# Rotary embedding on one core: two stores move from ScalarE's DMA ring to SyncE's

## The chip, the core and the metric

The kernel runs on one NeuronCore of a Trainium2 chip. The metric is the device time of one execution in microseconds, as a median over runs. A profile of one execution gives the span on the core, which is shorter than the device time by what lies around it.

The engines that matter here are ScalarE (ACT in the profile), VectorE (DVE) and SyncE (SP). SyncE does no arithmetic; it issues DMAs. ScalarE and SyncE each have a DMA ring of their own: q10 is ScalarE's, q1 is SyncE's. Both rings are served by the same 16 DMA engines.

## What is computed

```python
def reference(x, cos, sin, num_heads):      # x: 16 x 512 x 1024 f32, 16 heads
    x = x.reshape(batch, seq, num_heads, head_dim)          # head_dim 64
    x1, x2 = x[..., :half_dim], x[..., half_dim:]           # half_dim 32
    cos = cos[None, :, None, :]                             # 512 x 32
    sin = sin[None, :, None, :]
    rotated = np.concatenate([x1 * cos - x2 * sin,
                              x1 * sin + x2 * cos], axis=-1)
    return rotated.astype(np.float32)
```

The input has 33.55 MB and the output as much. The two tables are 64 KB each.

## The kernel before

The 16 batches are cut into 8 slabs of 4.19 MB. A slab lies in the on-chip memory as 128 partitions of 8192 f32 values (32 KB a partition). The tile `room` has 6 such slots, and slab s uses slot s modulo 6, so slabs 6 and 7 reuse the slots of slabs 0 and 1.

**Loads.** The dictionary `loads` lists six DMAs: loads 0, 1, 6 and 7 bring one slab each, loads 2 and 4 bring two (2 and 3, 4 and 5). A one-slab DMA moves 32 KB rows and a two-slab DMA 64 KB rows. All are issued by SyncE (line 71). Loads 0, 1, 2 and 4 are issued at the start. Load 6 may only be issued when store 0 has landed, because it overwrites slab 0's slot; load 7 likewise after store 1.

**Stores.** The dictionary `stores` lists seven: stores 0, 1, 2, 3, 6 and 7 of one slab and store 4 of two (4 and 5). All are issued by ScalarE (line 174), each after the last copy back of its slabs. In the source, the loads that the store makes room for follow right behind it in the same loop body.

**Tables.** The cosine and sine tables come in through ScalarE's ring (line 87), are spread over the partitions by eight small matmuls (line 128), and end as bf16 tables `tab` (line 133).

**Compute.** A pass is a slab, or half a slab for slabs 0, 6 and 7. In each pass ScalarE casts the slab in place from f32 to bf16 (line 144), VectorE makes two products with the tables (line 165) and their sum (line 168), and ScalarE copies the sum back to f32 into the slot (line 170). The cast of the next pass stands in the source ahead of the copy back of the present one, so the cast of a slab can hold up the copy back, and so the store, of the slab before it.

**Order.** The program that results keeps one instruction stream for each engine. Each stream is in a fixed order, though not always in the source's: in the trace ScalarE casts slab 1 before it copies slab 0 back, and it issues store 2 behind the cast of slab 4. An instruction that waits holds up all that stands behind it on its engine. DMAs of one ring are worked off in the order in which they were issued.

Of the kernel before, what the change touches and what calls it, by code (L numbers as in the profile page):

```python
# [2 lines left out]

# [4 lines left out]


@with_exitstack  # L10
def kernel(
    ctx: ExitStack,
    tc: tile.TileContext,
    x: bass.AP,
    cos: bass.AP,
    sin: bass.AP,
    num_heads: int,
    out: bass.AP,
):
    nc = tc.nc  # L20
    P = nc.NUM_PARTITIONS

    batch, seq, dim = x.shape
    nh = num_heads
    hd = dim // nh
    half = hd // 2
    bf16 = mybir.dt.bfloat16
    f32 = mybir.dt.float32

    nb = 2  # L30
    slots = 6
    nslabs = batch // nb
    G = 2
    rpp = nb * seq // P
    W = rpp * dim
    SP = seq // rpp
    TW = rpp * half

    out_flat = out.rearrange("b s h d -> b s (h d)")

    singles = ctx.enter_context(tc.tile_pool(name="singles", bufs=1))
    psum = ctx.enter_context(tc.tile_pool(
        name="psum", bufs=1, space=bass.MemoryType.PSUM))


    def dram(t, s, k):
        return bass.AP(tensor=t.tensor,
                       offset=t.offset + s // G * (G * nb * seq * dim) + s % G * W,
                       ap=[[G * W, P], [1, k * W]])


    def view(t, offset, *dims):
        return dataclasses.replace(t, offset=t.offset + offset,
                                   ap=[t.ap[0], *[list(d) for d in dims]])


    room = singles.tile([P, slots * W], f32, tag="room")
    halves = room.bitcast(bf16)


    def slab(s, k):
        return view(room, s % slots * W, (1, k * W))


    loads = {0: 1, 1: 1, 2: 2, 4: 2, 6: 1, 7: 1}
    stores = {0: 1, 1: 1, 2: 1, 3: 1, 4: 2, 6: 1, 7: 1}


    def load(s):
        k = loads[s]  # L70
        nc.sync.dma_start(out=slab(s, k), in_=dram(x, s, k))  # L71

    TR = 32
    TQ = seq // TR // rpp
    TC = seq * half // TR
    raw = singles.tile([P, TC], f32, tag="raw")
    nc.vector.memset(raw, 0.0)  # L79


    def load_tables(queue):
        for i, src in enumerate((cos, sin)):
            to = dataclasses.replace(
                raw, offset=raw.offset + i * raw.ap[0][0],
                ap=[[P // TR * raw.ap[0][0], TR], [1, TC]])
            queue.dma_start(out=to, in_=bass.AP(
                tensor=src.tensor, offset=src.offset, ap=[[TC, TR], [1, TC]]))


    load(0)
    load_tables(nc.scalar)
    for s in loads:
        if 0 < s < slots:
            load(s)

    GP = SP // G
    GT = G // TQ  # L100
    pick = singles.tile([P, 3 * GT * P], bf16, tag="pick")
    nc.gpsimd.memset(pick, 0.0)  # L102


    def selection(g, h):
        return pick[:, (g * GT + h // TQ) * P:(g * GT + h // TQ + 1) * P]


    for g in range(3):
        for h in range(0, G, TQ):  # L110
            part = view(selection(g, h), 0, (GP, P // GP), (1, GP))
            nc.gpsimd.affine_select(  # L112
                out=part, in_=part, compare_op=mybir.AluOpType.not_equal,
                fill=-1.0 if g == 2 else 1.0,
                base=-(1 if g else 0) - h // TQ * (P // TR),
                pattern=[[0, P // GP], [-(G // TQ) * (P // TR), GP]],
                channel_multiplier=1)

    raw_b = singles.tile([P, TC], bf16, tag="raw_b")
    nc.gpsimd.tensor_copy(out=raw_b, in_=raw)  # L120

    tab = {}


    def table(h):
        acc = psum.tile([P, 2 * rpp * hd], f32, tag=f"acc{h}")
        for g, at in ((0, 0), (0, half), (2, rpp * hd), (1, rpp * hd + half)):
            nc.tensor.matmul(  # L128
                view(acc, at, (hd, rpp), (1, half)), selection(g, h),
                view(raw_b, h % TQ * TW, (half, rpp), (1, half)),  # L130
                start=True, stop=True)
        tab[h] = singles.tile([P, 2 * rpp * hd], bf16, tag=f"tab{h}", name="tab")
        nc.vector.tensor_copy(out=tab[h], in_=acc)  # L133

    def span(u):
        s, r, n = u
        at, m = s % slots * W + r * dim, n * dim
        return (m, view(room, at, (1, m)), view(halves, 2 * at, (1, m)),
                view(halves, 2 * at + m, (1, m)))


    def cast(u):
        m, full, low, high = span(u)
        nc.scalar.copy(out=low, in_=full)  # L144

    passes = []
    for s in range(nslabs):  # L150
        n = rpp if 1 <= s < nslabs - 2 else rpp // 2
        passes += [(s, r, n) for r in range(0, rpp, n)]


    cast(passes[0])
    for i, u in enumerate(passes):
        s, r, n = u
        if s < G and r == 0:
            table(s)
        if i + 1 < len(passes):  # L160
            cast(passes[i + 1])
        m, full, low, high = span(u)
        turned = view(low, half, (hd, n * nh), (-half, 2), (1, half))
        for out_, in_, a in ((high, turned, rpp * hd), (low, low, 0)):
            nc.vector.tensor_mul(  # L165
                out=out_, in0=in_,
                in1=view(tab[s % G], a + r * hd, (hd, n), (0, nh), (1, hd)))
        nc.vector.tensor_add(out=high, in0=low, in1=high)  # L168

        nc.scalar.copy(out=full, in_=high)  # L170
        if r + n == rpp:
            for t, k in stores.items():
                if t + k - 1 == s:
                    nc.scalar.dma_start(out=dram(out_flat, t, k), in_=slab(t, k))  # L174
                    for v in range(t + slots, t + k + slots):
                        if v in loads:
                            load(v)


# [1 line left out]
_INS = ['x', 'cos', 'sin', 'num_heads']  # L181
_OUTS = [((16, 512, 16, 64), 'float32')]

_NUMBERS = {'num_heads': 16}


# [26 lines left out]
```

## Time and profile before

| what | value |
|---|---|
| median of 3 runs | 162.29 us (162.16 to 162.79) |
| the profiled execution, device time | 162.28 us |
| its span | 160.5 us |
| ScalarE cast f32 to bf16, whole slab (L144) | 7.02 us |
| ScalarE copy back, whole slab (L170) | 7.01 us |
| ScalarE, half a slab, either | 3.60 us |
| VectorE, the two products and the sum of a slab (L165, L168) | 8.88 and 4.43 us |
| loads issued by SyncE | 0.74, 1.16, 1.64, 2.10 (loads 0, 1, 2, 4), 70.21 (6), 90.72 (7) |
| loads, us from issue to landing | 12.6, 21.7, 43.3, 71.7, 23.7, 23.0 |
| stores issued by ScalarE | 36.93, 58.88, 73.86, 87.77 (0 to 3), 115.17 (4), 129.35 (6), 143.52 (7) |
| stores, us from issue to landing | 33.2, 31.8, 35.0, 33.2, 25.1, 20.6, 16.1 |

Times of issue are microseconds from the span's start. A DMA's landing is its issue plus the time to landing; a DMA that stands in a ring behind others counts that queueing as part of it. In the profile's lines an item such as "ACT room L144 <- DMA room<-in_x_dram: 20.9, 4, 9.4" means that line 144 on ScalarE waited for the load of x, 20.9 us in total, 4 times, 9.4 us at most. The row "DMA" of the page gives the busy share of the 16 DMA engines in 40 equal slices of the span, in tenths.

### The profile page before, as it was taken

What the parts mean: (1) busy time and instruction counts of PE and PEld (TensorE: products, weight loads), DVE (VectorE), ACT (ScalarE), POOL (GpSimd) and SP (SyncE); (2) the same over time, 40 slices, a digit from 0 to 9 for tenths busy, and PEclk for the clock granted to TensorE, in tenths of its full rate; (3) what the DMA queues carried; (4) which work ended last, traced back from release to release, by engine and by line L of the source; (5) the groups of instructions that cost most, each with busy time, mean ns of one, the idle gap of its engine ahead of it and who ended that gap; (6) DMA issues with size and microseconds to landing.
All of it is one profiled execution on the core that took longest, in us unless ns stands there. A gap on an engine that the chain in (4) does not pass through costs nothing.

```text
span 160.5 us, 162 instructions
## 1 busy us (share of the span) xinstructions
PE 1.9 (1%) x8; PEld 1.1 (1%) x8; DVE 109.9 (68%) x36; ACT 113.3 (71%) x23; POOL 2.1 (1%) x9
## 2 busy tenths in 40 slices
PE   0004000000000000000000000000000000000000
PEld 0002000000000000000000000000000000000000
DVE  1002999999900999899789989999649999800000
ACT  3006939991089999997999999929999999170000
POOL 3001000000000000000000000000000000000000
DMA  7999999969599999999999999999996996999994
GB/s 261 408 408 392 523 392 523 506 278 523 245 408 392 555 490 392 392 392 392 465 441 400 433 474 400 433 474 400 408 604 294 523 490 294 400 474 433 392 474 180
DMA packets 1968, 67.24 MB, mean 419 GB/s; under 512 B 240, under 2 KB 240, under 8 KB 304
## 3 DMA queue, kind: packets, MB, share of 16 engines
q1 hardware_dynamic: 864, 33.55, 49.4%
q10 hardware_dynamic: 1104, 33.69, 48.6%
HBM read 33.69 MB, written 33.55 MB: 419 GB/s over the span
## 4 chain that ended last, share of the span: by engine, by line
ACT 36%; DMA 27%; DVE 13%; issue 12%; another core or an unknown queue 1%; SPq 0%; ACTq 0%
DMA room<-in_x_dram 27%; ACT room L170 22%; ACT room L144 14%; DVE room L165 8%; DVE room L168 4%; SPq L71 0%; ACTq L174 0%; ACTq L170 0%
## 5 line engine op out<-in xcount | busy, mean ns | idle before, releaser
L165 DVE TENSOR_TENSOR room<-room,tab 128x4096 bf16<-128x4096 bf16 (+1 forms) x22 | 71.6, 3259 | 15.0 <-ACT room L144 14.6
L144 ACT CAST room<-room 128x4096 bf16<-128x4096 f32 (+1 forms) x11 | 56.6, 5153 | 20.9 <-DMA room<-in_x_dram 20.9
L170 ACT CAST room<-room 128x4096 f32<-128x4096 bf16 (+1 forms) x11 | 56.6, 5154 | 6.6 <-DVE room L168 6.6
L168 DVE TENSOR_TENSOR room<-room 128x4096 bf16<-128x4096 bf16 (+1 forms) x11 | 35.9, 3261 | 0.3
L133 DVE CAST tab<-acc 128x1024 bf16<-128x1024 f32 x2 | 2.4, 1219 | 13.6 <-PE acc L128 13.6
L144 ACT ACT_TABLE_LOAD x1 | 1.3, 1283 | 2.7 <-issue 2.7
L128 PE MATMUL acc<-raw_b,pick 128*128 128x256 bf16 x8 | 1.9, 415 | 13.9 <-POOL raw_b L120 13.9
L128 PEld LDWEIGHTS <-pick 128*128 128x128 bf16 x8 | 1.1, 140 | 14.2 <-issue 12.2
L79 DVE MEMSET raw<- 128x512 f32 x1 | 0.5, 485 | 0.9 <-PEq L194 0.9
L112 POOL TENSOR_SCALAR_AFFINE_SELECT pick<-pick 128x128 bf16<-128x128 bf16 x3 | 0.8, 309 | 0.1
L120 POOL CAST raw_b<-raw 128x512 bf16<-128x512 f32 x1 | 0.6, 610 | 11.2 <-DMA raw<-in_sin_dram 11.2
L102 POOL MEMSET pick<- 128x384 bf16 x1 | 0.4, 418 | 0.3 <-POOLq L194 0.3
L194 POOL MEMSET const-float32-0.0<- 128x1 f32 x1 | 0.1, 98 | 0.2 <-issue 0.2
L194 POOL MEMSET const-bfloat16-1.0<- 128x1 bf16 x1 | 0.1, 101 | 0.0
L194 POOL MEMSET const-uint8-127<- 128x1 uint8 x1 | 0.1, 101 | 0.0
L194 POOL MEMSET const-float32-1.0<- 128x1 f32 x1 | 0.1, 98 | 0.0
## 6 DMA issues: line engine op xcount, KB each, us to landing
out_dram<-room ACTq DMA_DIRECT2D x6, 4096.0 KB, 32.5
room<-in_x_dram SPq DMA_DIRECT2D x4, 4096.0 KB, 22.3
raw<-in_cos_dram ACTq DMA_DIRECT2D x1, 64.0 KB, 7.9
raw<-in_sin_dram ACTq DMA_DIRECT2D x1, 64.0 KB, 11.1
room<-in_x_dram SPq DMA_DIRECT2D x2, 57.5
out_dram<-room ACTq DMA_DIRECT2D x1, 25.1
```

Of the source, the lines that this page charges most:

```text
L79: nc.vector.memset(raw, 0.0)
L102: nc.gpsimd.memset(pick, 0.0)
L112: nc.gpsimd.affine_select(out=part, in_=part, compare_op=mybir.AluOpType.not_equal, fill=-1.0 if g == 2 else 1.0, base=-(1 if g else 0) - ...
L120: nc.gpsimd.tensor_copy(out=raw_b, in_=raw)
L128: nc.tensor.matmul(view(acc, at, (hd, rpp), (1, half)), selection(g, h), view(raw_b, h % TQ * TW, (half, rpp), (1, half)), start=True, sto ...
L133: nc.vector.tensor_copy(out=tab[h], in_=acc)
L144: nc.scalar.copy(out=low, in_=full)
L165: nc.vector.tensor_mul(out=out_, in0=in_, in1=view(tab[s % G], a + r * hd, (hd, n), (0, nh), (1, hd)))
L168: nc.vector.tensor_add(out=high, in0=low, in1=high)
L170: nc.scalar.copy(out=full, in_=high)
L194: nc = _bacc.Bacc("TRN2", target_bir_lowering=False, num_devices=1)
```

## The change

Stores 0 and 1 are issued by SyncE in place of ScalarE, so that they enter SyncE's ring behind loads 0, 1, 2 and 4. The other five stores remain with ScalarE. Loads 6 and 7 still follow in SyncE's ring, each still waiting until the store of its slot has landed.

```diff
@@ -171,7 +171,8 @@
         if r + n == rpp:
             for t, k in stores.items():
                 if t + k - 1 == s:
-                    nc.scalar.dma_start(out=dram(out_flat, t, k), in_=slab(t, k))
+                    queue = nc.sync if t < 2 else nc.scalar
+                    queue.dma_start(out=dram(out_flat, t, k), in_=slab(t, k))
                     for v in range(t + slots, t + k + slots):
                         if v in loads:
                             load(v)
```

No instruction is added or removed, and the bytes moved are the same.

## The prediction

> **What bounds the kernel now.** I read the page's rows over time first, then the DMA queues in windows, the timeline around the last slabs, the waits and the DMA issues.
>
> ```profile
> span 160.5 us, 162 instructions
> PE 1.9 (1%) x8; PEld 1.1 (1%) x8; DVE 109.9 (68%) x36; ACT 113.3 (71%) x23; POOL 2.1 (1%) x9
> ...
> DMA  7999999969599999999999999999996996999994
> ...
> HBM read 33.69 MB, written 33.55 MB: 419 GB/s over the span
> ```
>
> No engine is busy for more than 71% of the span, but the DMA row stands at 9 nearly throughout. A slab is 4.19 MB. Store 6 was issued at 129.35 and landed 20.6 us later, at 149.95; store 7 at 143.52 and 16.1 us, so 159.62. So a slab takes 9.67 us when nothing is beside it (434 GB/s). From load 0's landing (0.74 + 12.6 = 13.3) the remaining 62.9 MB at 434 GB/s end at 158.4, and the last store landed at 159.6: the DMA lost 1.2 us in all, and the digit 5 (slice 40.1 to 44.1 us, just after the first store's issue at 36.9) says where. The kernel is bound by bytes; what can change the time is whether the DMA engines run dry.
>
> How the two rings share, by the DMA view in two windows (queue, packets, MB, share): 46 to 68 us, then 76 to 92 us. q1 is SyncE's ring, q10 ScalarE's.
>
> ```profile
> q1 hardware_dynamic: 96, 6.29, 65.9%
> q10 hardware_dynamic: 96, 3.15, 33.1%
> ```
> ```profile
> q1 hardware_dynamic: 112, 3.67, 53.1%
> q10 hardware_dynamic: 112, 3.15, 45.5%
> ```
>
> Packets alternate one for one: 96 to 96 while loads 2 and 4 (two slabs, 64 KB rows) meet one-slab stores (32 KB rows), so the load takes two thirds; 112 to 112 where both have 32 KB rows, about half each. With both rings at work a slab needs 2 x 9.67 = 19.3 us.
>
> The timeline where slabs 4 to 6 pass (start, us, line):
>
> ```profile
> 94.57 7.01 ACT L170 CAST room<-room 128x8192 f32<-128x8192 bf16 x1
> 94.69 8.88 DVE L165 TENSOR_TENSOR room<-room,tab 128x8192 bf16<-128x8192 bf16 x2 [0.49 <-ACT room L144]
> 101.49 3.60 ACT L144 CAST room<-room 128x4096 bf16<-128x4096 f32 x1
> 103.61 4.43 DVE L168 TENSOR_TENSOR room<-room 128x8192 bf16<-128x8192 bf16 x1
> 107.95 4.61 DVE L165 TENSOR_TENSOR room<-room,tab 128x4096 bf16<-128x4096 bf16 x2
> 108.12 7.02 ACT L170 CAST room<-room 128x8192 f32<-128x8192 bf16 x1 [3.04 <-DVE room L168]
> ...
> 115.17 0.34 ACTq L174 DMA_DIRECT2D out_dram<-room  x1
> ```
>
> ScalarE's order here is: copy back slab 4 (L170), cast the first half of slab 6 (L144), copy back slab 5, issue store 4 (slabs 4 and 5). The cast of slab 6 needs load 6 and stands in front of store 4. It waits for nothing now: load 6 was issued at 70.21 and landed 23.7 us later, at 93.9. Store 4 reaches its ring at 115.17, and store 3 ahead of it lands at 87.77 + 33.2 = 121.0: 5.8 us in hand.
>
> What waits, engines first, then SyncE:
>
> ```profile
> ACT room L144 <- DMA room<-in_x_dram: 20.9, 4, 9.4
> ```
> ```profile
> SPq L71 <- DMA out_dram<-room: 87.4, 2, 67.3
> ```
>
> SyncE issues four loads by 2.8 us and then sits: load 6 waits for store 0 (landed 36.93 + 33.2 = 70.1), load 7 for store 1 (58.88 + 31.8 = 90.7).
>
> **The change, part by part.**
>
> Two issues leave ScalarE and go to SyncE. Each took 0.34 us of ScalarE's sequencer at 36.93 and 58.88; after the first ScalarE waits for load 2 until 44.91 anyway, the second runs under a cast. Removing them is worth 0, and SyncE has idle time for two issues of 0.33 to 0.7 us. On SyncE the wait for slab 0's copy back now stands before store 1, load 6 and load 7, which all need it or come later.
>
> Loads 2 and 4 lose their competitor. Load 1 landed at 22.86; two slabs more give load 2 at 42.2 (before 44.9) and load 4 at 61.5 (before 73.8). ScalarE follows: cast of slab 2 at 42.2, copy back of slab 1 until 56.1 (store 1 can be issued 2.8 us earlier), cast of slab 3 until 63.1, copy back of slab 2 until 70.0, store 2 issued at 70.0 (before 73.86). The compute gains about 3.9 us here, which nothing at the end needs.
>
> Store 0 starts behind load 4 and has the engines alone: it lands at 61.5 + 9.7 = 71.2 (before 70.1). Load 6 is issued then, 1.1 us later than before. That is not its price: store 1 has been in SyncE's ring since 56.1 and stands ahead of it, while store 2, then store 3 (issued by 84), fill ScalarE's ring. From 71.2 each ring moves two slabs at 19.3 us: SyncE's store 1 and load 6, ScalarE's stores 2 and 3. All end at about 71.2 + 38.7 = 109.9. **Load 6 lands at 109.9 instead of 93.9.** This is the step that costs.
>
> ScalarE would come to the cast of slab 6 at about 98 (101.5 less the gain) and waits 12 us for load 6. Behind it on ScalarE stand the copy back of slab 5, whose data VectorE has by 105, and store 4; VectorE waits too. Cast 109.9 to 113.4, copy back to 120.4, store 4 issued at 120.4 (before 115.2), its first packets some 1.2 us later: 121.6. (No packet moved in the first microsecond, 6 did from 1.0 to 1.9 and 9 more to 2.4, after load 0's issue at 0.74.) Meanwhile the only work left is load 7: after load 6 it needs 9.7 us, so its data end at 118.9 (landing 119.6; I estimate 0.7 us from data to landing, as the 434 GB/s run into 159.6 leaves it). **The DMA runs dry from 118.9 to 121.6, 2.7 us.** Bounds: 0, if SyncE's ring gets some 7% more than half so that load 6 is early and store 3 is left over for the gap; 3.3, if first packets come 1.6 us after the issue (upper end of load 0's row) and the landing costs 0.2 more. I take 2.7, since both windows above show equal packets.
>
> After the gap stores 4, 6 and 7 run back to back: store 6 would be issued near 134.5 and store 7 near 148.6, before their predecessors end (141 and 150.6). Nothing makes up for the gap.
>
> The 1.2 us of loss at 40 to 44 is uncertain. Either it belongs to the first store of all (it then stays, near 61) or to a store ring starting against a load in flight (it then vanishes, as store 0 now follows loads in their own ring, unless store 2's start costs the same). Bounds 0 and -1.2; no row tells them apart, so I take -0.6.
>
> Sum: 160.5 + 2.7 - 0.6 = 162.6 us of span. The profiled execution took 162.28, 1.8 around its span, and the median is 162.29: **164.4 us**. Own range 163.2 to 165.5.
>
> **The rivals.**
>
> *The ring does not matter.* Total bytes and rate are fixed, and 429 and 426 GB/s moved in windows whether two-slab loads or stores were the partner. If load 6 lands by 107 (its cast then frees store 4 for 118.9), the engines never run dry: 162.3. For it: 5.8 us were in hand. Against it: load 6 has 16 us of extra queueing. The Trainium skill, "DMA: Bandwidth & Descriptors", section "Issuing engines are not separate DMA queues", speaks for this rival: DMAs of all issuing engines run on the same 16 engines and interleave, and choosing another issuer only saves sequencer time. By it the sum would be 162.3. The trace agrees on the rate; the order within a ring is what the rule says nothing of.
>
> *Faster.* The 1.2 us vanish and load 6 lands by 107: 162.3 - 1.2 = 161.1. It decides at the same point, 2.7 us less for load 6, and needs the loss to belong to two rings meeting.
>
> *Another order of instructions.* ScalarE's order in the trace is not the source's (the cast of slab 1 starts at 22.86, before the copies of slab 0 at 29.79), so the new program's order is a guess. If SyncE gets store 0, load 6, store 1, load 7, as the source's loop reads, store 1 is issued only after store 0 landed, lands near 110, and load 7 follows only then, beside store 4 with its 64 KB rows: 8 rounds of 3.63 us (1.21 + 2.42) put load 7 at some 141. From the cast of slab 7 (122.06) to store 7 (143.52) it is 21.5 us, then about 12 for a lone store as for load 0: 174.5, time 177. If instead ScalarE copies slab 5 back before it casts slab 6, store 4 meets load 7 in the same way, and the end is near 172.5, time 175. Against the first: the change as described puts both stores behind four loads and loads 6 and 7 after them. Against the second: it needs ScalarE's order to change, though only SyncE's instructions move.
>
> **How the numbers follow.** Forecast 0.70 (164.4); the ring does not matter 0.11 (162.3); faster 0.08 (161.1); another order 0.11 (175 to 177). The range goes down to include the neutral case, and up beyond the forecast's own; it leaves out the other orders and most of the faster case: 161.8 to 166.5. About 0.5% (0.8 us) is what a measurement of this kernel can tell from no change. Faster: 0.08 and a little of the neutral case, 0.09. Same: 0.10 of the neutral case and 0.04 of the forecast's low end, 0.14. Slower: the rest, 0.77.
>
> **What would show it.** Load 2 landing near 42, load 4 near 61.5, store 0 near 71. SyncE issuing store 1 at 56 and load 6 at 71. Load 6 landing near 110, and the cast of slab 6 (L144) idle for about 12 us before it, released by the load. Store 4 issued near 120.4, and the DMA row with a lower digit in the slice at 118 to 122. Wrong is the prediction if load 6 lands before 107, if SyncE's order differs, or if store 4 is issued before that cast.

## The result and the profile after

| kernel | median of the runs | ratio to before, 95% interval | span of the profiled execution |
|---|---|---|---|
| before | 162.29 us (162.13 to 162.79, 7 runs) | | 160.5 us |
| changed | 162.88 us (162.77 to 163.06, 7 runs) | 1.0036 [1.0026, 1.0045] | 161.2 us |

The change costs 0.6 us, which the interval sets clearly apart from nothing, though it is under the 0.5% that was named as the least this kernel's measurement can tell. The forecast was 164.4.

The page of the changed kernel, with the lines that answer to those of before: the DMA row, the bytes, then the two waits.

```profile
span 161.2 us, 165 instructions
...
DMA  7999999969969996999999999999989969999996
...
HBM read 33.69 MB, written 33.55 MB: 417 GB/s over the span
```
```profile
ACT room L144 <- DMA room<-in_x_dram: 12.0, 2, 9.6
```
```profile
SPq L71 <- DMA out_dram<-room: 30.6, 2, 21.0
```

The bytes are the same. The page counts 165 instructions instead of 162: the three more are waits for semaphores, one on SyncE and two on ScalarE, and the arithmetic and the DMAs are unchanged. The 5 that stood at 40 to 44 us has gone; a 6 stands at 44 to 48 us and another at 60 to 64 us, and an 8 at 117 to 121 us. A single low digit says little while 64 KB packets are counted by their start; the windows below decide. ScalarE waits less for loads (12.0 instead of 20.9 us in total). There is no 12 us wait in front of the cast of slab 6. The timelines of ScalarE say why. Before, from the cast of slab 2 to the copy back of slab 2:

```profile
44.91 7.02 ACT L144 CAST room<-room 128x8192 bf16<-128x8192 f32 x1 [8.02 <-DMA room<-in_x_dram]
51.84 7.01 ACT L170 CAST room<-room 128x8192 f32<-128x8192 bf16 x1
...
58.76 7.01 ACT L144 CAST room<-room 128x8192 bf16<-128x8192 f32 x1
...
65.68 7.01 ACT L170 CAST room<-room 128x8192 f32<-128x8192 bf16 x1
```

The changed kernel, from the copy back of slab 1 to the issue of store 4, with three rows of VectorE that the copies back of slabs 2 and 3 wait for:

```profile
44.30 7.02 ACT L170 CAST room<-room 128x8192 f32<-128x8192 bf16 x1 [7.25 <-DVE room L168]
51.22 20.85 ACT L144 CAST room<-room 128x8192 bf16<-128x8192 f32 x3
58.27 13.22 DVE L165 TENSOR_TENSOR room<-room,tab 128x8192 bf16<-128x8192 bf16 x3 [14.06 <-ACT room L144]
71.41 4.42 DVE L168 TENSOR_TENSOR room<-room 128x8192 bf16<-128x8192 bf16 x1
...
75.91 7.02 ACT L170 CAST room<-room 128x8192 f32<-128x8192 bf16 x1 [3.84 <-DVE room L168]
80.19 4.42 DVE L168 TENSOR_TENSOR room<-room 128x8192 bf16<-128x8192 bf16 x1
...
84.70 7.02 ACT L170 CAST room<-room 128x8192 f32<-128x8192 bf16 x1 [1.77 <-DVE room L168]
84.73 7.36 ACTq L175 DMA_DIRECT2D out_dram<-room  x2
92.14 7.02 ACT L144 CAST room<-room 128x8192 bf16<-128x8192 f32 x1 [0.41 <-ACT room L170]
...
105.98 7.11 ACT L144 CAST room<-room 128x4096 bf16<-128x4096 f32 x2
...
112.99 7.01 ACT L170 CAST room<-room 128x8192 f32<-128x8192 bf16 x1
...
120.04 0.34 ACTq L175 DMA_DIRECT2D out_dram<-room  x1
```

Before, ScalarE alternated: cast slab 2, copy slab 1 back, cast 3, copy 2 back, cast 4 and store 2, and so on. Now it copies slab 1 back first, at 44.30, then casts slabs 2, 3 and 4 in one go (51.22 to 72.07), and only then copies slabs 2 and 3 back. VectorE gets slab 2 later for it and begins at 58.27 (before at 51.96); it makes the two products of slab 2 and one of slab 3 before the sum of slab 2 (71.41), where before that sum followed its own products. So the copy back of slab 2 starts at 75.91, when the sum is done, 3.84 us after the last of the three casts. Store 2 stands behind the copy back of slab 3 as well and is issued at 84.73, just after the sum of slab 3 is done (80.19 + 4.42 = 84.61). Stores 2 and 3 are issued at 84.73 and 91.75 instead of 73.86 and 87.77. Moving two DMAs to another engine has thus changed the order of two engines whose arithmetic the diff does not touch; why the new order came out so is not shown. SyncE's order is the forecast's: loads 0, 1, 2, 4, stores 0 and 1, loads 6 and 7.

Four answers of the DMA view, each of a window around one issue, in the changed kernel: load 6 (issued at 72.70), load 7 (82.78), store 2 (84.73) and store 4 (120.04). The last number is the time to landing.

```profile
room<-in_x_dram SPq DMA_DIRECT2D x1, 4096.0 KB, 23.1
...
room<-in_x_dram SPq DMA_DIRECT2D x1, 4096.0 KB, 32.4
...
out_dram<-room ACTq DMA_DIRECT2D x1, 4096.0 KB, 23.2
...
out_dram<-room ACTq DMA_DIRECT2D x1, 20.8
```

With store 2 at 84.73, store 1 had the engines to itself and landed at 51.34 + 31.4 = 82.7. Load 6 followed at once and landed at 95.8, not at 109.9 as forecast. Store 4 needed 20.8 us to land: two slabs alone take 2 x 9.67 = 19.3, so next to nothing was ahead of it. Before it needed 25.1 us, because store 3 was still under way. This is a sign that the DMA engines may have run dry; the windows show it.

Where the time went is seen in the DMA columns of the windows (last two numbers: busy share, GB/s). They count a packet in the window in which it starts: GB/s times the window's length gives the bytes started, and share times length the time that those packets took on each of 16 engines. Before, then the changed kernel:

```profile
36.00:38.00 2.00, 0.00 (x0) 0.00 (x0) 2.00 (x1) 0.90 (x1) 0.00 (x0) 1.00 1.21 524
...
39.00:42.00 3.00, 0.00 (x0) 0.00 (x0) 2.97 (x2) 0.00 (x0) 0.00 (x0) 1.00 1.20 350
```
```profile
58.00:59.00 1.00, 0.00 (x0) 0.00 (x0) 0.73 (x1) 1.00 (x2) 0.00 (x0) 1.00 3.72 1049
...
120.00:120.85 0.85, 0.00 (x0) 0.00 (x0) 0.85 (x1) 0.85 (x2) 0.00 (x0) 1.00 0.01 0
120.85:122.00 1.15, 0.00 (x0) 0.00 (x0) 1.15 (x2) 1.15 (x1) 0.00 (x0) 1.00 2.14 912
```

Each of the first three windows holds 1.05 MB, 16 packets of 64 KB, one for each engine. In the first they took 1.21 x 2 = 2.42 us, in the second 1.20 x 3 = 3.60, in the third 3.72. So the last load packets ahead of the first store are stretched by 1.2 us before and 1.3 us after: the stretch has moved with the first store, from 39 to 58 us, and has not vanished. In the window from 120.00 to 120.85 of the changed kernel next to no packet starts. Packets of store 3 that started earlier still run in it; behind them the engines wait for store 4's first packets, 0.31 us on the mean.

From the packets' records I add up, for the kernels of this table, how much longer than usual the packets took (usual is 1.21 us for 32 KB and 2.42 for 64 KB) and how long engines had no packet, as a mean over 16 engines. The first microseconds and the last are left out. The labels e1 to e10 are the experiments of the next section.

| kernel | stretched, us | no packet, us | both, less before | span, less before |
|---|---|---|---|---|
| before | 1.20 | 0 | 0 | 0 |
| changed | 1.39 + 0.26 (near 87) | 0.31 (near 121) | +0.8 | +0.6 |
| e1, rings new, order old | 1.17 | 1.52 (near 121) | +1.5 | +1.3 |
| e2, rings old, order new | 1.16 | 3.55 (near 122) | +3.5 | +3.5 |
| e4, store 4 sooner | 1.5 | 2.45 (near 151) | +2.7 | +2.6 |
| e8, store 0 alone, order old | 1.25 | 0 | 0 | -0.1 |
| e9, as e1, store 2 later | 1.16 | 0 | 0 | -0.2 |
| e10, as e1, store 4 first | 1.6 | 5.82 (near 140 and 153) | +6.2 | +6.0 |

The two sums give each span to about 0.2 us. For the changed kernel they are 0.31 us without a packet and 0.45 us of longer packets, against 0.6 us of span. So the question for each kernel is where the DMA engines run dry, and where packets are stretched.

### The profile page after: what moved, and what is told of

Read it like the earlier page. It is cut to its first block, busy times and chain, and to the rows that moved or that the text cites. A ratio compares the mean times of both kernels' runs of the same rounds, so it can differ in the third digit from the quotient of the medians.

```text
span 161.2 us, 165 instructions
## 1 busy us (share of the span) xinstructions
PE 1.9 (1%) x8; PEld 1.1 (1%) x8; DVE 109.0 (68%) x36; ACT 113.4 (70%) x23; POOL 2.1 (1%) x9
## 4 chain that ended last, share of the span: by engine, by line
DVE 50%; ACT 26%; DMA 7%; issue 5%; PE 1%; ACTq 1%; POOLq 0%; DVEq 0%
DVE room L165 36%; ACT room L170 15%; DVE room L168 12%; ACT room L144 11%; DMA raw<-in_sin_dram 7%; DVE tab L133 1%; PE acc L128 1%; POOLq L209 0%; ACTq L87 0%; DVE raw L79 0%; ACTq L175 0%; ACTq L170 0%; POOLq L120 0%; DVEq L165 0%
## 5 line engine op out<-in xcount | busy, mean ns | idle before, releaser
L165 DVE TENSOR_TENSOR room<-room,tab 128x4096 bf16<-128x4096 bf16 (+1 forms) x22 | 71.2, 3257 | 17.2 <-ACT room L144 17.0
L128 PE MATMUL acc<-raw_b,pick 128*128 128x256 bf16 x8 | 1.9, 415 | 14.1 <-POOL raw_b L120 14.1
## 6 DMA issues: line engine op xcount, KB each, us to landing
out_dram<-room ACTq DMA_DIRECT2D x1, 20.8
```

What stands on the lines that cost most here:

```text
L128: nc.tensor.matmul(view(acc, at, (hd, rpp), (1, half)), selection(g, h), view(raw_b, h % TQ * TW, (half, rpp), (1, half)), start=True, sto ...
L165: nc.vector.tensor_mul(out=out_, in0=in_, in1=view(tab[s % G], a + r * hd, (hd, n), (0, nh), (1, hd)))
```

## The experiments

All timed runs are compared with the kernel before on the same chip. To hold an order, the instructions are given names and each is told to stand behind the one ahead of it in a list, without a wait. Holding an order costs nothing that can be seen: e8 and e9 hold one and take 162.2 us. In these kernels the lines are three further down: L147 is the cast, L173 the copy back, L74 the load, L178 the store. In the lists c is a cast, y a copy back, S a store; the digits are the slab and the row where the pass begins.

**e1: the new rings with the old order.**

```diff
+    for row in ('c00 c04 c10 y00 y04 c20 y10 c30 y20 c40 S2 y30 c50 S3 y40 c60 y50 c64 S4 ...',
+                'L0 L1 L2 L4 S0 S1 L6 L7', ...):
+        row = row.split()
+        for a, b in zip(row, row[1:]):
+            tc.add_manual_dep(did[b].ins, did[a].ins.name, ...)
```

> The changed kernel with ScalarE's and VectorE's instructions held in the order of the kernel before (stores 0 and 1 on SyncE, store 2 again behind the cast of slab 4, the cast of slab 6 in front of the copy back of slab 5). Theory (the prediction's queueing is right, but it needs ScalarE's old order, which the changed kernel no longer has): store 2 issued near 70, load 6 lands near 111, the cast of slab 6 waits more than 10 us, store 4 is issued at 120.5 to 122, the DMA engines stand still for about 2 us before it; time 164.0 to 165.0. Rival (the ring does not matter, only bytes do): 162.3 to 162.9, no gap.

Measured: 163.57 us, ratio 1.0082 [1.0069, 1.0095]. The timeline of this kernel, around slab 6:

```profile
110.20 3.60 ACT L147 CAST room<-room 128x4096 bf16<-128x4096 f32 x1 [12.58 <-DMA room<-in_x_dram]
113.71 7.01 ACT L173 CAST room<-room 128x8192 f32<-128x8192 bf16 x1
...
120.75 0.34 ACTq L178 DMA_DIRECT2D out_dram<-room  x1
```

Load 6 landed at 72.47 + 37.7 = 110.2, the cast waited 12.58 us for it, the copy back of slab 5 stood behind the cast, and store 4 came at 120.75. This is the chain of the prediction, with load 6 and store 4 each within 0.4 us of its figures. The engines had no packet for 1.5 us, not 2.7. The time is 0.4 us below the range expected, and the rival (162.3 to 162.9) is refuted. So the queueing was right for the order it assumed, and with the new rings that order is dearer than the changed kernel's.

**e2: the old rings with the new order.** All stores remain with ScalarE; the list is that of the changed kernel.

```diff
+            'c00 c04 c10 y00 y04 S0 y10 c20 S1 c30 c40 y20 y30 S2 S3 c50 y40 c60 c64 y50 c70 S4 ...'
```

> All stores on ScalarE as before, but ScalarE and VectorE in the order that the changed kernel has (casts of slabs 2, 3 and 4 ahead of the copies back of slabs 2 and 3). Theory (order and rings act together: with the old rings the cast of slab 4 waits for load 4 until 73.7, and all behind it comes late): store 2 issued near 87, store 4 near 122 to 123, about 2 us without DMA before it; time 164.3 to 165.8. Rival 1 (the order itself is what cost 0.6 us, and the rings nothing): 162.9. Rival 2 (neither matters): 162.3.

Measured: 165.79 us, ratio 1.0216 [1.0203, 1.0229], at the upper edge of what the theory expected; both rivals (162.9 and 162.3) are refuted. The engines had no packet for 3.5 us, more than the 2 us expected. Its timeline:

```profile
73.66 7.02 ACT L147 CAST room<-room 128x8192 bf16<-128x8192 f32 x1 [8.68 <-DMA room<-in_x_dram]
...
87.63 7.26 ACTq L178 DMA_DIRECT2D out_dram<-room  x2
```

With stores 0 and 1 competing, load 4 lands at 73.6 and the cast of slab 4 waits 8.68 us for it; in this order the copies back of slabs 2 and 3 stand behind that cast. In the changed kernel load 4 landed at 2.09 + 60.8 = 62.9 and no such wait is there. The four corners are therefore 162.3 (old, old), 163.6 (rings new), 165.8 (order new) and 162.9 (both new). Each half costs alone, +1.3 and +3.5 us, and together they cost only 0.6: the new order fits the new rings.

**e9: e1 with store 2 alone moved back.**

```diff
-            '... y20 c40 S2 y30 c50 S3 ...'
+            '... y20 c40 y30 c50 S2 S3 ...'
```

> As the run with both stores on SyncE and ScalarE's old order, with one thing changed: store 2 stands behind the cast of slab 5, so that it is issued near 84 instead of 70, as in the changed kernel. Theory (what the changed kernel's new order gave back is that store 2 comes late, so that store 1 has the DMA engines alone and load 6 comes early): load 6 lands near 96 instead of 110, the cast of slab 6 waits for nothing, store 4 is issued near 111, no gap near 121, time 162.1 to 162.6. Rival (it is the new order of the casts of slabs 2 to 4 that gave it back): 163.6 as with the old order.

Measured: 162.18 us, ratio 0.9996 [0.9987, 1.0005]. Store 2 was issued at 76.52, not at 84: the copy back of slab 3 (from 76.75) and the cast of slab 5 (from 83.67) stand ahead of it, but ScalarE's queue had passed both as soon as their data were there, while the engine was still at work on the cast of slab 4 (69.83 to 76.84). It is 6.5 us later than in e1 all the same. The timeline:

```profile
76.52 0.35 ACTq L178 DMA_DIRECT2D out_dram<-room  x1
...
103.86 3.60 ACT L147 CAST room<-room 128x4096 bf16<-128x4096 f32 x1 [6.25 <-DMA room<-in_x_dram]
107.37 7.01 ACT L173 CAST room<-room 128x8192 f32<-128x8192 bf16 x1
...
114.42 0.34 ACTq L178 DMA_DIRECT2D out_dram<-room  x1
```

Load 6 landed at 103.8 (6.4 us earlier than in e1), store 4 was issued 6.3 us earlier, and no engine ran dry. All of e1's 1.3 us came back by this one place, with the casts of slabs 2 to 4 in their old order. The expected figures for load 6 (96) and store 4 (111) were missed with the issue, and a wait of 6.25 us remained in front of the cast, which costs nothing, as store 4 still came before its turn in the ring. The rival (163.6) is refuted: it is the time at which store 2 starts to share, not the casts as such, that decides when load 6 lands.

**e8: store 0 alone goes to SyncE, old order.**

```diff
-                    queue = nc.sync if t < 2 else nc.scalar
+                    queue = nc.sync if t in (0,) else nc.scalar
```

> Store 0 alone goes to SyncE, store 1 stays with ScalarE, ScalarE and VectorE in the order of the kernel before. Theory (the loss comes from where load 6 stands in the queue: here one store less is ahead of it than with both stores moved, and two-thirds shares no longer hold it up): load 6 lands near 106, store 4 is issued near 117, sooner than store 3's end, no gap, time 162.2 to 162.6. Rival (moving any store to SyncE's ring costs, by the stretch or the ring switch): 162.7 to 163.2.

Measured: 162.24 us, ratio 0.9999 [0.999, 1.0008]. Load 6 landed at 107.1, and store 4 was issued at 117.66, while load 7 was still under way (landed at 120.9), so nothing ran dry. The theory's figures were met but for one: store 3 had already landed at 83.94 + 32.1 = 116.0, and it was load 7 that kept the engines busy until store 4. A store in SyncE's ring costs nothing by itself, and load 6 may land as late as 107 without harm, which is where the prediction had set that point.

**e10: e1 with the copy back of slab 5 ahead of the cast of slab 6.**

```diff
-            '... y40 c60 y50 c64 S4 ...'
+            '... y40 y50 c60 S4 c64 ...'
```

> As the run with both stores on SyncE and ScalarE's old order, with the copy back of slab 5 in front of the first cast of slab 6, so that store 4 need not wait for load 6. Theory (store 4's 64 KB rows then run beside load 7 with its 32 KB rows, packet by packet, so load 7 gets a third): store 4 issued near 111, load 7 lands near 133, store 7 is issued near 154, about 5 us without DMA at the end, time 167 to 169; the prediction's figure for this order was 175. Rival (the wait of the cast for load 6 is the whole loss): 162.3.

Measured: 168.47 us, ratio 1.0380 [1.0366, 1.0394]. Load 7 was issued at 90.61 and landed at 133.2; store 7 was issued at 154.57. Windows near the end (DMA columns last):

```profile
152.00:155.40 3.40, 0.00 (x0) 0.00 (x0) 0.00 (x0) 2.54 (x1) 0.00 (x0) 1.00 0.00 0
155.40:157.00 1.60, 0.00 (x0) 0.00 (x0) 0.00 (x0) 0.00 (x0) 0.00 (x0) 1.00 1.54 655
```

No packet starts in 3.4 us, since store 6 is done and store 7's first packets come only after its issue at 154.57. The figures of this run's theory were met. This is the mechanism of the prediction's rival "another order", in its second form: store 4's long rows beside load 7 slow it. Its price was too high: 175 was forecast and 168.5 measured.

**e4 and e5: closing the changed kernel's own gap.** In e4 the copy back of slab 5 stands between the two casts of slab 6; in e5 the cast of slab 5 stands ahead of the copy back of slab 3.

```diff
-            '... y20 y30 S2 S3 c50 y40 c60 c64 y50 c70 S4 ...'
+            '... y20 y30 S2 S3 c50 y40 c60 y50 c64 S4 c70 ...'
```
```diff
-            '... y20 y30 S2 S3 c50 y40 c60 c64 y50 c70 S4 ...'
+            '... y20 c50 S2 y30 S3 y40 c60 c64 y50 c70 S4 ...'
```

> The changed kernel in its own order, but with the copy back of slab 5 in front of the second cast of slab 6, so that store 4 is issued about 0.4 us sooner. Theory (0.3 us of the loss is the DMA standing still between store 3's end and store 4's first packets): the gap near 121 shrinks to 0.1 or less, time 162.5 to 162.7. Rival (the loss of the change lies in the stretched packets at 58 to 62 and 87 alone): 162.9, as the changed kernel.

> The changed kernel in its own order, but with ScalarE's cast of slab 5 moved in front of the copy back of slab 3, since VectorE waited 1.3 us for it. Theory (the gap of 0.3 us before store 4 is part of the loss, and nothing later has less slack than that): store 4 issued near 119 instead of 120.04, no DMA gap near 121 and none later, time 162.4 to 162.7. Rival (the change's loss is the stretched packets alone): 162.9.

Measured: e4 164.89 us, ratio 1.0162 [1.0149, 1.0175]; e5 162.91 us, ratio 1.0041 [1.0028, 1.0054]. Both closed the gap near 121, and both missed the time expected. e4 issued store 4 at 119.44 but delayed the second cast of slab 6. VectorE's order, held as in the changed kernel, wants that cast before it makes the first sum of slab 6, so stores 6 and 7 came 6.2 us later than in the changed kernel, and the engines ran dry for 2.4 us ahead of store 7. The edit opened a later gap; it says that store 7 had less than 6.2 us in hand, and nothing about the 0.3 us. e5 issued store 4 at 118.68 and had no gap anywhere, but the engines ended at different times (0.7 us without a packet in the last two microseconds, 0.4 before) and the packets near 85 were stretched by 0.4 us. Its six runs fall into two groups, 162.72 to 162.74 and 163.07 to 163.31, and the profile is of the second, so the median 162.91 stands for neither; that it equals the rival's 162.9 proves nothing. The 0.3 us of the gap was not clearly recovered, and whether it can be is open.

**e3, e6 and e7: the stretch ahead of the first store.** e3 and e6 issue one more, tiny store, at the head of ScalarE's ring or later; e7 stores slab 0 in halves.

```diff
+    first = singles.tile([P, 128], f32, tag="first")
+    nc.gpsimd.memset(first, 0.0)
+    nc.scalar.dma_start(out=bass.AP(tensor=out_flat.tensor,
+        offset=dram(out_flat, 7, 1).offset, ap=[[G * W, P], [1, 128]]), in_=first)
```
```diff
+        if s == 0:
+            h = dram(out_flat, 0, 1)
+            did[f"H{r * 2 // rpp}"] = nc.sync.dma_start(
+                out=dataclasses.replace(h, offset=h.offset + r * dim, ap=[h.ap[0], [1, W // 2]]),
+                in_=view(room, r * dim, (1, W // 2)))
```

> The kernel before, with one more store of 64 KB (zeros into the place of slab 7, which store 7 overwrites) at the head of ScalarE's ring, issued before the tables. The stretch of 1.2 us of the last load packets ahead of the first store (at 39 to 43 us before, 58 to 62 in the changed kernel). Theory A (it belongs to the first store of the program, whichever it is): it moves to the first microseconds or vanishes, no stretched packets near 40; time 161.0 to 162.3. Theory B (it belongs to the first store that meets a stream of loads with long rows): it stays near 40, time 162.3 to 162.6.

> The kernel before in its own order, with one more store of 64 KB in 512-byte rows (zeros into the place of slab 7, which store 7 overwrites) on ScalarE between the copies back of slab 0's halves, so that the first store that meets a stream of loads is a tiny one. Theory A (the stretch of 1.2 us is paid once, by the first store packets that meet loads, and is as long as these packets take): the stretch near 40 falls to 0.4 us or less, time 161.2 to 161.8. Theory B (it is paid by the first slab-sized store, whatever went before): stretch of 1.2 us stays at 39 to 43, time 162.3 to 162.6.

> The changed kernel in its own order, with store 0 cut into two DMAs of half a slab each (16 KB rows), both in SyncE's ring. Theory A (the stretch at 58 to 62 us is as long as the first store packet takes, 1.2 us for 32 KB): it falls to about 0.6 us, time 162.1 to 162.5. Theory B (it does not depend on the packets of the first store): 1.2 to 1.4 us as in the changed kernel, time 162.8 to 163.1.

Measured: e3 163.23 us (161.97 to 164.08, 12 runs), ratio 1.0049 [1.0026, 1.0072]; e6 161.97 us, ratio 0.9982 [0.9974, 0.9991]; e7 162.71 us, ratio 1.0027 [1.0017, 1.0037]. In all three the stretch is there ahead of store 0: 1.1 us at 44 to 48 in e3, 1.0 us near 48 in e6, 1.1 us at 58 in e7 with its 16 KB rows. Neither a tiny store at the start, nor one among the loads, nor a first store of half the row length takes it away. The stretch thus follows theory B, but none of the three times fell into the range of either theory, and what the stretch is remains open. e3's time is no clean measure, as its early store held up the tables (landed at 21.7 instead of 13.1) and with them VectorE. e6 was issued at 26.3, earlier than meant, and its store crept beside the loads until 49.5, with store 0 behind it in the ring; loads 2 and 4 landed earlier (42.3 and 68.7 us), and the kernel is 0.2% faster than the one before, the only one here whose interval lies below 1.

## Why the prediction was wrong

**Right: the bound, the shares, SyncE.** The engines move about 434 GB/s whichever ring carries the bytes (a packet of 32 KB takes 1.21 us and one of 64 KB 2.42 us in either ring), and time is lost only where they run dry or where packets are stretched. SyncE's order was as assumed. Loads 2 and 4 landed at 1.62 + 40.7 = 42.3 (forecast 42.2) and 62.9 (61.5; the 1.3 us more is the stretch), and store 0 at 37.07 + 35.6 = 72.7 (71.2).

**Wrong, and the step that failed: "ScalarE follows: cast of slab 2 at 42.2, copy back of slab 1 until 56.1 ..., store 2 issued at 70.0".** It took ScalarE's old order for the changed program. In its place the profile shows a new order, in which the cast of slab 2 starts at 51.22, three casts in a row and VectorE's late sum stand ahead of the copy back of slab 2, and store 2 is issued at 84.73. Two steps rested on it. "From 71.2 each ring moves two slabs at 19.3 us" failed, since SyncE's ring was alone until store 2's first packet at 88.8, and "Load 6 lands at 109.9" became 95.8. e1 shows that with the old order the step holds (110.2), and e9 that store 2's start is what moves it. The prediction knew that ScalarE's order in the trace is not the source's, and it listed another order among its rivals, but it looked only at the place where store 4 and the cast of slab 6 meet, and held a new order unlikely because only SyncE's instructions move. That reason was wrong.

**Right by accident: store 4 at 120.4.** It was issued at 120.04, but for another reason: VectorE began slab 2 only at 58.27 in the new order (it had waited 14.1 us for the cast), the copy back of slab 3 waited for its sum until 84.70, and from there ScalarE worked with hardly a pause until 120.0, with both casts of slab 6 ahead of the copy back of slab 5. The engines ran dry for 0.31 us and not for 2.7, because store 3 kept them busy: it landed at 91.75 + 29.5 = 121.3, where the forecast had only load 7 left, landing at 119.6. That the measured 162.88 us lies within the stated range of 161.8 to 166.5 is luck too: the range reached down for the case in which nothing changes, not for a new order.

**Mis-sized even with its own order: "2.7 us" and "-0.6".** The sum for e1's kernel was +2.1 of span; it measured +1.3. The gap's start was put at 118.9, but load 7 landed at 90.80 + 30.0 = 120.8, 1.2 us later than forecast, and the gap was 1.5 us. The stretch accounts for the 1.2 us: it stays whole (1.17 in e1, where half of it was written off), load 6 was issued at 72.47 where 71.2 was forecast, and all work ahead of the gap ends later by as much. So the stretch must not be left out when the gap's start is worked out. Load 6 landed as forecast in spite of it, as a ring that joins while the other is busy starts late: store 2 was issued at 69.96 in e1 and its first packet started at 73.8, where the forecast had it sharing from 71.2.

**The rivals.** "The ring does not matter" came nearer to the measured time (162.3) than the forecast, but it is refuted as a reason: 1.3 us hang on the rings at the old order, and 2.9 us at the new one, with opposite signs. The Trainium skill, "DMA: Bandwidth & Descriptors", section "Issuing engines are not separate DMA queues", says that all issuers' DMAs interleave on the same engines; the trace agrees on the rate, and the runs show what the rule leaves out, that a ring's order decides which load lands first. "Faster" failed at both conditions: the stretch stayed, and the gap was not nil.

## What to carry to other kernels

When an instruction moves to another engine, read the order of every engine in the new program before costing the move; the old trace's order is an assumption with its own chance. In a kernel bound by bytes, add up where the DMA engines have no packet or slow ones: here that sum told the spans of the seven other kernels in the table to about 0.2 us (but not e5's, whose engines ended out of step). A store or load that comes late costs nothing until the engines run dry for want of it, so look for the place with the least slack (here store 4 and store 7), and work out the drain before it with every loss that lies ahead.

## What the runs showed that was not expected

The last load packets ahead of the first slab-sized store, 16 of them (27 in e3), cost 0.9 to 1.3 us more than usual on the mean of the engines, once in every kernel of this case: with the store in the other ring (3.60 instead of 2.42 us before) or in the loads' own ring (3.72 in the changed kernel). Its cause is open. A smaller one, of 0.2 to 0.4 us, comes later in the changed kernel, e4, e5 and e7 (packets of load 6, at 84 to 88 us) and in e10 (load 7, at 114 to 116 us): each time a load has the engines to itself and a newly issued store of ScalarE's ring is about to join. In the changed kernel it is 0.26 us of what the change costs, and it comes with the new order, which leaves load 6 alone until store 2 starts. It is no rule: in e8 store 4 joins load 7 in the same way without a stretch.

A ring that joins when the other is busy starts late: 5.6 us for store 0 before (issued at 36.93, first packet at 42.5, beside 64 KB rows), 3.8 us for store 2 in e1 and 4.1 us in the changed kernel (84.73, first packet at 88.8, beside 32 KB rows), 2.4 us for store 4 in e8 (117.66, first packet at 120.0, beside 32 KB rows too), against 0.85 us for store 4 of the changed kernel, which came to idle engines.
